# First layer's up and gate products of the feed-forward as block products, seven for eight

## The chip, the cores and the metric

One Trainium2 chip, one core. The metric is the device time of one launch in microseconds; the median of the runs counts.

## The reference, cut to what matters

Two layers over 256 context tokens and 512 latent tokens of width 1024, all in float32. In each layer a mixing sub-layer is followed by a feed-forward sub-layer:

```python
def swiglu(h, w_up, w_down):
    g, u = jnp.split(h @ w_up, 2, axis=-1)
    return (jax.nn.silu(g) * u) @ w_down
...
        x = post_norm(x, gate2 * swiglu(modulate(x, shift2, scale2), ffn_w_up[l], ffn_w_down[l]), ln2_g[l], ln2_b[l])
        if not last:
            xc = post_norm(xc, gate2c * swiglu(modulate(xc, shift2c, scale2c), ffn_w_up[l], ffn_w_down[l]), ln2_g[l], ln2_b[l])
```

`w_up` is 1024 x 5632 (gate columns, then up columns), `w_down` 2816 x 1024. In the first layer both token sets go through (768 tokens), in the last one only the latent tokens (512).

## The kernel before, in words

**Three matmuls for a product.** Every large operand is kept as two float32r tiles, hi (a rounded copy, made by ScalarE) and lo (the rest, made by VectorE). `mm3` (line 240) adds hi x hi, hi x lo and lo x hi in PSUM for each block of 128 along K. `wload` (208) brings weights into `wf` on the sync queue (SP), casts them into `wh` (219) and subtracts into `wl` (220); `wf` has two buffers, `wh` and `wl` four each, of up to 1056 columns. `wchunk` (224) loads 4 K blocks at a time.

**Feed-forward of layer 0** (lines 1486 to 1541). The input `h2` lies channel-major: 8 K blocks x 768 tokens, hi and lo. The hidden width is 22 tiles of 128, in three parts of 8, 7 and 7. For each tile `up` (1498) loads 128 gate and 128 up columns, and `cm` (265) makes, for the latent tokens (512 columns, `LG`) and the context tokens (256, `CG`), the gate product, then Silu on ScalarE (1505), the up product, the multiplication on VectorE (1507) and the hi/lo split into `a` (1509, 1510). After each part `to_tokens` (1254) makes its down products: four column quarters of `w_down`, six token tiles each, `a` as the stationary operand; VectorE multiplies by the gate row (1263) and adds to `X` (1265, 1267). In the last part the normalisation (`fin2`, `post`, `norm_mod`, `modulate`) of a token tile follows its last quarter, and the next layer's first weights are loaded.

**The first two tiles.** Their weights are loaded within the output product of the mixing sub-layer; they are done by column groups (latent first), as the normalised tokens arrive in the order 2, 3, 4, 5, 0, 1 (0 and 1 are context).

**Buffers.** PSUM banks of products alternate between two (`pl`) and three (`pq`) through `pw` (123). `u` (two buffers) holds the normalised tokens and then the gate activations; `lng`, `lnb`, `grow0`, `grow1` hold rows that are broadcast; `hf` (two) the modulated blocks.

**Order.** The code gives an order; the framework that builds the program orders each engine's and queue's instructions by a plan made ahead, taking an instruction when its inputs and buffers are free in that plan, so the order within an engine may differ from the code's. On the chip each engine goes through its own list in order. Modulation vectors of later stages (`ada`, 298, four matmuls and a 512 KB load of `wa` a piece) are slipped in by `pieces`, three per weight chunk in this stage (`NP[2]`).

Of the kernel before, what the change touches and what calls it, by code (L numbers as in the profile page):

```python
# [89 lines left out]
def block_kernel(ctx, tc, t, out, dbg=None):  # L90
# [17 lines left out]
    def nm(s):  # L108
        uid[0] += 1
        return f"{s}_{uid[0]}"  # L110
# [128 lines left out]

    def mm3(po, lhs, rhs):  # L240
        n = len(lhs)
        for k in range(n):
            (ah, al), (bh, bl) = lhs[k], rhs[k]
            mm(po, ah, bh, start=(k == 0), stop=False)  # L244
            mm(po, ah, bl, start=False, stop=False)  # L245
            mm(po, al, bh, start=False, stop=(k == n - 1))  # L246

# [113 lines left out]

    def gate_row(pool, l, which, s):

        g = pool.tile([P, D], F32, tag=f"grow{s}", name=nm("grow"), bufs=1)
# [45 lines left out]

    def modulate(tp, h, i, xhs, fs, nd=0):

        s = 1 if i < 2 else 0
        for k2 in range(0, KT, 2):
            hf = tp.tile([P, 2, 2 * P], F32, tag="hf", name=nm("hf"), bufs=2)
            po = pm().rearrange("p (k s) -> p k s", k=2)
# [836 lines left out]

    def to_tokens(pool, l, which, X, W_of, lhs_of, nk, tiles_, first, final, grows, fin, following):

        def part(t_, W, q):
            mark('w_out' if which == 1 else 'down')
            po = pw()[:, :256]
            mm3(po, lhs_of(t_), W)
            g = grows[1 if t_ < 2 else 0]  # L1260
# [11 lines left out]
        for q in range(2 if final else 4):  # L1272
            W = W_of(q)
            for t_ in tiles_:
# [141 lines left out]
    for l in range(DEPTH):  # L1416
# [7 lines left out]
        with tc.tile_pool(name=f"ff{l}", bufs=1, reuse_waits="tile") as fp:  # L1424
# [8 lines left out]
            for i in tiles_:  # L1433
# [5 lines left out]
                nc.sync.dma_start(X[i], src)  # L1439

            def rows_of(w):
                gr = fp.tile([P, D], F32, tag="lng", name=nm("lng"), bufs=1)
                br = fp.tile([P, D], F32, tag="lnb", name=nm("lnb"), bufs=1)
# [11 lines left out]
            def norm_mod(t_, hdst, f, z):  # L1455

                V = nc.vector
                xh = fp.tile([P, D], F32, tag="u", name=nm("xh"), bufs=2)
                V.tensor_scalar(z[:, 1:2], z[:, 0:1], -1.0 / D, None, op0=ALU.mult)
# [6 lines left out]
                if len(xhs) == 2:  # L1466
                    modulate(fp, hdst, t_ - 1, xhs, f, 4 if t_ in tiles_[-2:] else 0)
# [4 lines left out]
            grows = [gate_row(fp, l, 1, s) if not (last and s == 1) else None for s in range(2)]  # L1472

# [13 lines left out]
            ahead.update(n=NP[2], lim=(l + 1, 2))  # L1487
            gr, br = rows_of(2)
            grows = [gate_row(fp, l, 2, s) if not (last and s == 1) else None for s in range(2)]
            groups = [LG] if last else [LG, CG]  # L1490
            parts = [(0, 8), (8, 7), (15, 7)]
            hn = None
            for pi_, (k0, nk) in enumerate(parts):
                a = new_h(hpool)
                mark('up')
                Wu, ut = {}, {}

                def up(kk, gs_):
                    if kk not in Wu:
                        Wu[kk] = w_up(k0 + kk) if pi_ or kk > 1 else Wn[kk]  # L1500
                        ut[kk] = fp.tile([P, D], F32, tag="u", name=nm("sg"), bufs=2)
                    sg = {}
                    for po, g in cm(Wu[kk], 0, h2, gs_, pw):
                        sg[g] = ut[kk][:, g[0]:g[1]]
                        nc.scalar.activation(sg[g], po, AF.Silu)
                    for po, g in cm(Wu[kk], P, h2, gs_, pw):
                        nc.vector.tensor_tensor(sg[g], po, sg[g], op=ALU.mult)
                        hi = a.t[:, 0, kk, g[0]:g[1]]
                        nc.scalar.copy(hi, sg[g])
                        nc.vector.tensor_tensor(a.t[:, 1, kk, g[0]:g[1]], sg[g], hi.bitcast(F32), op=ALU.subtract)  # L1510
                if pi_ == 0:

                    for g in ((NC_, 512), (512, NT)) + (() if last else (CG,)):
                        up(0, [g])
                        up(1, [g])
                for kk in range(0 if pi_ else 2, nk):
                    up(kk, groups)
                if not last and pi_ == 1:
                    ada_to(l + 1, 2)
                    fsn = shift_scale(l + 1, 1)  # L1520
                if pi_ == 1:
                    ahead["n"] = 0
                final = pi_ == 2
                if final and not last:
                    hn_box = []

                def fin2(t_, st):
                    mark('fin2')
                    z = None if last else sm.tile([P, 5], F32, tag="z", name=nm("z"))
                    post(t_, gr, br, st, None if last else z[:, 0:1])  # L1530
                    if last:
                        nc.sync.dma_start(out[0, (t_ - 2) * P:(t_ - 1) * P, :], X[t_])
                    else:
                        if t_ >= 2:
                            nc.sync.dma_start(xdram[(t_ - 2) * P:(t_ - 1) * P, :], X[t_])
                        if not hn_box:
                            hn_box.append(new_h(hpool2))
                        norm_mod(t_, hn_box[0], fsn, z)
                Wn = to_tokens(fp, l, 2, X, lambda q: wchunk(t["ffn_w_down"][l], [(q * 256, 256)], r0=k0 * P, nk=nk),
                               lambda t_: a.sl(t_ * P, (t_ + 1) * P, 0, nk), nk, tiles_, pi_ == 0, final, grows, fin2,  # L1540
                               lambda n: None if last else wchunk(t["w_in"][l + 1], [((O_AQ, O_AFF)[n], 256)]))
        hg.__exit__(None, None, None)
        if not last:
            h, hg, hpool = hn_box[0], hg2, hpool2

# [31 lines left out]
```

## Time and profile before

| what | us |
|---|---|
| median of 3 runs | 2526.88 (2523.86 to 2527.05) |
| the profiled execution, its own time | 2528.81 |
| its span, first to last instruction | 2526.9 |
| PE busy in the span | 2463.4 (97%) |
| VectorE busy | 1348.1 (53%) |
| ScalarE busy | 875.3 (35%) |
| GpSimd busy | 140.6 (6%) |

PE is the tensor engine, DVE VectorE, ACT ScalarE, POOL GpSimd, SP the sync engine. The profile's page gives busy shares, the chain of work that ended last, and groups of instructions by line. The mean granted clock of PE is 0.992 of full speed. Matmuls overlap, so the spacing of their starts, not the printed length, is what each takes from PE.

### The profile page before, as it was taken

To read this page: it belongs to the slowest core of one execution; us is meant where nothing else is said; L and a number is where in the kernel's file an instruction comes from. 1 tells how busy PE (TensorE), PEld (TensorE's weight loads), DVE (VectorE), ACT (ScalarE), POOL (GpSimd) and SP (SyncE) were. 2 spreads that over 40 slices of the span, in tenths; PEclk is the share of its full clock that TensorE was granted. 3 is DMA by queue.
4 is the path that set the end of the run, shared out by engine and by line. 5 is a ranking of instruction groups with operands and counts; after the bars stand their busy time and mean duration, and the time that the engine had idled before them with its cause. 6 is when DMAs were issued, how large, how long until landed. Compare 5 with 4: busy or idle time off the path is not lost.

```text
span 2526.9 us, 41389 instructions
## 1 busy us (share of the span) xinstructions
PE 2463.4 (97%) x17088; PEld 2108.2 (83%) x17088; DVE 1348.1 (53%) x2896; ACT 875.3 (35%) x1549; POOL 140.6 (6%) x214
## 2 busy tenths in 40 slices
PE   7999999999999999999999999999999999999998
PEld 5878889788678988998998988778887688898987
DVE  4477575445449652232332474768566577443436
ACT  3435553333332242212212144456343423322221
POOL 2000000100100120000000040000010102000000
PEclk9999999999999999999999999999999999999999
DMA  7453122112236444122122164421313265423332
GB/s 247 137 171 118 55 69 80 61 61 97 72 103 202 167 138 145 58 68 67 56 71 59 56 195 142 128 80 59 105 51 112 76 204 184 120 84 101 92 98 78
DMA packets 251936, 269.54 MB, mean 107 GB/s; under 512 B 14972, under 2 KB 219876, under 8 KB 251748
## 3 DMA queue, kind: packets, MB, share of 16 engines
q1 hardware_dynamic: 236867, 238.69, 30.8%
q10 hardware_dynamic: 14880, 28.21, 3.0%
q8 instruction: 134, 2.20, 0.4%
q14 instruction: 55, 0.44, 0.0%
HBM read 238.28 MB, written 26.48 MB: 105 GB/s over the span
## 4 chain that ended last, share of the span: by engine, by line
PE 89%; DVE 4%; DMA 2%; ACT 2%; issue 1%; POOL 1%; SPq 1%; POOLq 0%; ACTq 0%; DVEq 0%
PE pl L244 18%; PE pl L246 17%; PE pl L245 17%; PE pq L245 8%; PE pq L244 8%; PE pq L246 8%; PE po L311 2%; PE po L954 1%; PE pm L942 1%; DMA wa<-in_ada_w_dram 1%; PE pq L1168 1%; PE po L1001 1%; PE pq L1072 1%; DMA wf<-in_w_in_dram 1%; PE pm L989 1%
## 5 line engine op out<-in xcount | busy, mean ns | idle before, releaser
L244 PE MATMUL pl<-h,wh 128*128 128x512 f32 (+1 forms) x1720 | 623.7, 363 | 7.9 <-ACT s L925 2.5
L245 PE MATMUL pl<-h,wh 128*128 128x512 f32 (+1 forms) x1720 | 618.2, 360 | 0.0
L246 PE MATMUL pl<-h,wl 128*128 128x512 f32 (+1 forms) x1720 | 618.1, 359 | 0.0
L220 DVE TENSOR_TENSOR wl<-wf,wh 128x1024 fp32r<-128x1024 f32 (+2 forms) x288 | 348.1, 1209 | 354.0 <-ACT wh L219 339.0
L219 ACT CAST wh<-wf 128x1024 fp32r<-128x1024 f32 (+2 forms) x288 | 298.5, 1037 | 529.2 <-PE pq L246 232.3
L244 PEld LDWEIGHTS pl<-h,wh 128*128 128x128 f32 x1720 | 326.6, 190 | 73.3 <-issue 12.6
L246 PEld LDWEIGHTS pl<-h,wl 128*128 128x128 f32 x1720 | 326.4, 190 | 57.8 <-issue 10.1
L245 PEld LDWEIGHTS pl<-h,wh 128*128 128x128 f32 x1720 | 327.0, 190 | 50.8 <-issue 6.9
L244 PE MATMUL pl<-wh,h 128*128 128x256 f32 (+1 forms) x1048 | 296.2, 283 | 0.6 <-ACT dtr L521 0.4
L245 PE MATMUL pl<-wl,h 128*128 128x256 f32 (+1 forms) x1048 | 296.1, 283 | 0.0
L246 PE MATMUL pl<-wh,h 128*128 128x256 f32 (+1 forms) x1048 | 296.0, 283 | 0.0
L246 PE MATMUL pq<-h,wl 128*128 128x256 f32 (+1 forms) x680 | 219.5, 323 | 0.0
L244 PE MATMUL pq<-h,wh 128*128 128x256 f32 (+1 forms) x680 | 219.3, 323 | 0.0
L245 PE MATMUL pq<-h,wh 128*128 128x256 f32 (+1 forms) x680 | 218.6, 322 | 0.0
L244 PEld LDWEIGHTS pl<-wh,h 128*128 128x128 f32 x1048 | 198.0, 189 | 4.6 <-issue 2.3
L245 PEld LDWEIGHTS pl<-wl,h 128*128 128x128 f32 x1048 | 198.0, 189 | 3.8 <-issue 3.2
L246 PEld LDWEIGHTS pl<-wh,h 128*128 128x128 f32 x1048 | 198.1, 189 | 3.5 <-issue 3.3
L245 PE MATMUL pq<-wl,h 128*128 128x256 f32 x600 | 168.9, 282 | 0.0
L246 PE MATMUL pq<-wh,h 128*128 128x256 f32 x600 | 168.6, 281 | 0.0
L244 PE MATMUL pq<-wh,h 128*128 128x256 f32 x600 | 168.6, 281 | 0.0
L244 PEld LDWEIGHTS pq<-h,wh 128*128 128x128 f32 x680 | 128.0, 188 | 14.1 <-issue 2.6
L245 PEld LDWEIGHTS pq<-h,wh 128*128 128x128 f32 x680 | 128.3, 189 | 13.6 <-issue 1.8
(419 smaller groups left out, 3483.2 us busy)
## 6 DMA issues: line engine op xcount, KB each, us to landing
wf<-in_w_in_dram SPq DMA_DIRECT2D x120, 512.0 KB, 3.5
wa<-in_ada_w_dram SPq DMA_DIRECT2D x96, 512.0 KB, 3.9
wf<-in_ffn_w_up_dram SPq DMA_DIRECT2D x176, 256.0 KB, 3.1
wf<-in_ffn_w_down_dram SPq DMA_DIRECT2D x32, 512.0 KB, 3.3
gsp<-gs ACTq DMA_DIRECT2D x32, 384.0 KB, 2.5
gld<-gsp SPq DMA_DIRECT2D x16, 768.0 KB, 4.8
wf<-in_w_branch_dram SPq DMA_DIRECT2D x16, 512.0 KB, 3.4
wf<-in_w_out_dram SPq DMA_DIRECT2D x16, 512.0 KB, 3.9
```

Of the source, the lines that this page charges most:

```text
L219: nc.scalar.copy(wh[:, :a * b], wf[:, :a * b])
L220: nc.vector.tensor_tensor(wl[:, :a * b], wf[:, :a * b], wh[:, :a * b].bitcast(F32), op=ALU.subtract)
L244: mm(po, ah, bh, start=(k == 0), stop=False)
L245: mm(po, ah, bl, start=False, stop=False)
L246: mm(po, al, bh, start=False, stop=(k == n - 1))
L311: mm(po[32 * j:32 * j + 32, :], cT[:, k].rearrange("p r s -> p (r s)"), wf[:, j * 256:(j + 1) * 256], start=(k == 0), stop=(k == KT - 1))
L942: nc.tensor.transpose(pt[:, (2 * k + j) * P:(2 * k + j + 1) * P], x, ident)
L954: mm(po[hh * 64:hh * 64 + 64, :], va(hh, k), PT[hh][k], start=(k == 0), stop=(k == nk - 1))
L989: nc.tensor.transpose(pt[:, (2 * k + j) * P:(2 * k + j + 1) * P], Pj[j][:, (2 * b + k) * P:(2 * b + k + 1) * P], ident)
L1001: mm(po[hh * 64:hh * 64 + 64, cs], va(hh, k) if k < 2 else va(hh, k - 2, i2 + j), PT[hh][k][:, cs], start=(k == 0), stop=(k == 3))
L1072: mm(out_, q3[rows, u, i * P:(i + 1) * P], k3[rows, u, c0:c1], start=True, stop=True)
L1168: mm(out_, qS[rows, u, i * P:(i + 1) * P], kS[rows, u, c0:c1], start=True, stop=True)
```

## The change

Only layer 0's feed-forward changes in what it computes with; layer 1 keeps its code. Hidden tiles 0 and 1 are made as before. For tiles 2 to 21, two at a time (`k`, `k + 1`), the gate product and then the up product of 256 columns x 1024 x 768 tokens are split into 2 x 2 blocks (128 columns, 512 of K, 384 tokens) and made by `seven`: seven block products instead of eight, with sums of weight blocks before (in place in a raw float32 tile, `w8`), and sums of products after. `split` makes hi and lo of one 512-element block; two of them share a `wh`/`wl` buffer. The four sums of input blocks, `T`, are made once by `t_sums`; one of them replaces the block of `h2` that is not used by itself. The result of each pair (after Silu and multiplication) is stored to a DRAM tile `ad` from the GpSimd queue and read back by `bring` on the SP queue, which makes hi and lo, before and during the down products. The down parts are 8, 8 and 6 tiles long; the first begins with the first four K blocks of four token tiles (`begun`). Gate rows and normalisation rows share the `w8` buffers; the gate rows of the second sub-layer are made at the start of the down products instead of ahead of the up products. One piece of a modulation vector follows each group of seven. `modulate` takes halves of one `hf` tile.

The core of the diff:

```diff
+    def split(x):
+        if pair["n"] % 2 == 0:
+            pair["h"] = wt.tile([P, WN], F32R, tag="wh", name=nm("wh"), bufs=4)
+            pair["l"] = wt.tile([P, WN], F32R, tag="wl", name=nm("wl"), bufs=4)
+        c = 512 * (pair["n"] % 2)
+        pair["n"] += 1
+        hi, lo = (pair[q][:, c:c + 512].rearrange("p (k c) -> p k c", k=4) for q in "hl")
+        nc.scalar.copy(hi, x)
+        nc.vector.tensor_tensor(lo, x, hi.bitcast(F32), op=ALU.subtract)
+        return [(hi[:, k], lo[:, k]) for k in range(4)]
+
+    def t_sums(x, B, T):
...
+        whole(x1, 12)
+        whole(x2, 22)
+        V.tensor_tensor(x3, x2, x1, op=ALU.subtract)
+        put(3, x3)
+        whole(x3, 11)
+        V.tensor_tensor(x1, x1, x3, op=ALU.subtract)
+        put(1, x1)
+        V.tensor_tensor(x2, x2, x1, op=ALU.subtract)
+        put(2, x2)
+        whole(x3, 21)
+        V.tensor_tensor(x3, x2, x3, op=ALU.subtract)
+        put(4, x3)
+
+    def seven(raw, F, cp, out_):
+        V, A = nc.vector, nc.scalar
+        n = cp[0].shape[-1]
+        a11, a12, a21, a22 = (raw[:, 4 * k:4 * k + 4, m * P:(m + 1) * P] for m in range(2) for k in range(2))
+        p1, u2, u3, p5 = cp
+
+        def product(L, name):
+            po = pw()[:, :n]
+            mm3(po, L, F[name])
+            return po
+        L1 = split(a11)
+        A.copy(p1, product(L1, "11"))
+        L22 = split(a22)
+        V.tensor_tensor(a22, a21, a22, op=ALU.add)
+        A.copy(p5, product(split(a22), "t1"))
+        V.tensor_tensor(a21, a11, a21, op=ALU.subtract)
+        V.tensor_tensor(a11, a22, a11, op=ALU.subtract)
+        V.tensor_tensor(u2, p1, product(split(a11), "t2"), op=ALU.add)
+        L3 = split(a21)
+        z = product(L22, "t4")
+        V.tensor_tensor(u3, u2, product(L3, "t3"), op=ALU.add)
+        V.tensor_tensor(u2, u2, p5, op=ALU.add)
+        V.tensor_tensor(out_[3], u3, p5, op=ALU.add)
+        V.tensor_tensor(out_[2], u3, z, op=ALU.subtract)
+        L4 = split(a12)
+        V.tensor_tensor(out_[0], p1, product(L4, "21"), op=ALU.add)
+        V.tensor_tensor(a12, a12, a11, op=ALU.subtract)
+        V.tensor_tensor(out_[1], u2, product(split(a12), "22"), op=ALU.add)
...
+            def w8():
+                return fp.tile([P, 2 * D], F32, tag="w8", name=nm("w8"), bufs=2)
...
+                def store(k, sg):
+                    nc.gpsimd.dma_start(ad[k:k + 2].rearrange("k p s -> p k s"), sg)
...
+                for k in range(2, HID // P, 2):
+                    mark('up')
+                    sg = hidden()
+                    s4 = sg.rearrange("p k (n s) -> p (k n) s", n=2)
+                    for gu in range(2):
+                        raw = raw_of(k, gu) if gu or k > 2 else raw0
+                        cp = fp.tile([P, 2 * NT], F32, tag="hf", name=nm("cp"), bufs=1)
...
+                        seven(raw, F, c4, c4 if gu else [s4[:, q] for q in range(4)])
+                        for m in range(2):
+                            if not gu:
+                                nc.scalar.activation(sg[:, m], sg[:, m], AF.Silu)
+                            else:
+                                nc.vector.tensor_tensor(sg[:, m], cp[:, m * NT:(m + 1) * NT], sg[:, m], op=ALU.mult)
+                        pieces(ahead["n"], ahead["lim"])
+                    store(k, sg)
...
+                def bring(dst, n, k, tl):
+                    mark('down')
+                    st_ = tl()[:, :2 * NT].rearrange("p (k s) -> p k s", k=2)
+                    nc.sync.dma_start(st_, ad[k:k + 2].rearrange("k p s -> p k s"))
+                    hi = dst.t[:, 0, n:n + 2]
+                    nc.scalar.copy(hi, st_)
+                    nc.vector.tensor_tensor(dst.t[:, 1, n:n + 2], st_, hi.bitcast(F32), op=ALU.subtract)
+                parts = [(h2, 0, 8), (T_, 8, 8), (h2, 16, 6)]
+                for n, tl in zip(range(0, 8, 2), (u_tile, w8, w8, u_tile)):
+                    bring(h2, n, n, tl)
+                grows = gate_rows(2)
```

## Rows read from the trace of the kernel before

**Rows 1.** Part 1 of the page: busy time of each engine

```profile
PE 2463.4 (97%) x17088; PEld 2108.2 (83%) x17088; DVE 1348.1 (53%) x2896; ACT 875.3 (35%) x1549; POOL 140.6 (6%) x214
```

**Rows 2.** Part 4 of the page: the chain that ended last

```profile
PE 89%; DVE 4%; DMA 2%; ACT 2%; issue 1%; POOL 1%; SPq 1%; POOLq 0%; ACTq 0%; DVEq 0%
```

**Rows 3.** Table of stretches: us; PE, PEld, DVE, ACT, POOL busy; clock, DMA share, GB/s

```profile
1125.00:1250.00 125.00, 125.00 (x740) 110.59 (x740) 35.09 (x50) 29.34 (x44) 0.00 (x0) 1.00 0.22 65
...
1427.00:1500.00 73.00, 72.90 (x627) 66.75 (x626) 55.23 (x116) 25.38 (x38) 19.94 (x27) 1.00 0.46 147
```

**Rows 4.** Waits of PE, 905 to 1500 us: total, times, longest

```profile
PE po L311 <- DMA wa<-in_ada_w_dram: 3.2, 1, 3.2
```

**Rows 5.** Timeline of ACT: gate activations of second and third part, first and last

```profile
1131.48 0.60 ACT L1505 ACTIVATE sg<-pl 128x512 f32<-128x512 f32 x1 [4.46 <-PE pl L246]
...
1232.00 0.60 ACT L1505 ACTIVATE sg<-pl 128x512 f32<-128x512 f32 x1 [3.99 <-PE pl L246]
...
1308.80 0.60 ACT L1505 ACTIVATE sg<-pl 128x512 f32<-128x512 f32 x1 [4.54 <-PE pl L246]
...
1408.06 0.60 ACT L1505 ACTIVATE sg<-pl 128x512 f32<-128x512 f32 x1 [3.97 <-PE pl L246]
```

**Rows 6.** Timeline of PE, an up tile: from 512 columns to 256

```profile
1156.20 0.39 PE L246 MATMUL pl<-h,wl 128*128 128x512 f32 x1
...
1156.43 0.28 PE L244 MATMUL pq<-h,wh 128*128 128x256 f32 x1
...
1156.55 0.28 PE L245 MATMUL pq<-h,wh 128*128 128x256 f32 x1
```

**Rows 7.** Timeline of DVE, an up tile

```profile
1142.22 1.23 DVE L220 TENSOR_TENSOR wl<-wf,wh 128x1024 fp32r<-128x1024 f32 x1 [0.28 <-ACT wh L219]
1143.36 0.42 DVE L1507 TENSOR_TENSOR sg<-pq,sg 128x256 f32<-128x256 f32 x1
1143.70 1.22 DVE L220 TENSOR_TENSOR wl<-wf,wh 128x1024 fp32r<-128x1024 f32 x1
...
1156.70 0.69 DVE L1507 TENSOR_TENSOR sg<-pl,sg 128x512 f32<-128x512 f32 x1 [11.45 <-PE pl L246]
```

**Rows 8.** Timeline of ACT, the same up tile

```profile
1140.60 0.62 ACT L1509 CAST h<-sg 128x512 fp32r<-128x512 f32 x1 [5.91 <-DVE sg L1507]
...
1142.55 1.06 ACT L219 CAST wh<-wf 128x1024 fp32r<-128x1024 f32 x1 [0.36 <-PE pq L245]
1143.81 0.41 ACT L1509 CAST h<-sg 128x256 fp32r<-128x256 f32 x1 [0.21 <-DVE sg L1507]
1148.21 0.60 ACT L1505 ACTIVATE sg<-pl 128x512 f32<-128x512 f32 x1 [3.99 <-PE pl L246]
```

**Rows 9.** Table of stretches before and behind PE's wait (columns as in rows 3)

```profile
916.40:919.60 3.20, 0.06 (x4) 0.07 (x8) 0.00 (x0) 0.72 (x1) 0.00 (x0) 0.83 0.45 172
919.60:923.00 3.40, 3.40 (x21) 2.26 (x21) 0.55 (x1) 0.00 (x0) 0.00 (x0) 0.50 0.37 101
923.00:926.50 3.50, 3.50 (x28) 2.21 (x27) 2.33 (x4) 2.88 (x5) 1.24 (x2) 0.67 0.52 173
```

**Rows 10.** Timeline of DVE, end of the first sub-layer

```profile
922.45 1.18 DVE L424 TENSOR_SCALAR hf<-pm,modc,modc 128x256 f32<-128x256 f32 x2 [9.06 <-PE pm L420]
...
930.46 0.67 DVE L429 TENSOR_TENSOR h<-hf,h 128x512 fp32r<-128x512 f32 x1
...
951.28 0.42 DVE L1507 TENSOR_TENSOR sg<-pq,sg 128x256 f32<-128x256 f32 x1 [2.87 <-PE pq L246]
```

**Rows 11.** Timelines of SP and ACT queues: a gate load, the last gate store

```profile
715.45 0.89 SPq L1236 DMA_DIRECT2D gld<-gsp  x2
...
754.02 0.33 ACTq L1191 DMA_DIRECT2D gsp<-gs  x1
```

**Rows 12.** Tiles gsp (stored from ACT) and gld (loaded by SP): issue to landing, all

```profile
DMA to landing us min/median/max: 2.0/3.1/6.2
...
DMA to landing us min/median/max: 3.4/4.7/6.2
```

More of the change, by code (lines that the diff above doesn't have):

```diff
@@ L237, in wchunk, with mm3 @@
         return res
-    def mm3(po, lhs, rhs):
+    def mm3(po, lhs, rhs, first=True, final=True):
         n = len(lhs)
@@ L243, in mm3 @@
             (ah, al), (bh, bl) = lhs[k], rhs[k]
-            mm(po, ah, bh, start=(k == 0), stop=False)
+            mm(po, ah, bh, start=(first and k == 0), stop=False)
             mm(po, ah, bl, start=False, stop=False)
-            mm(po, al, bh, start=False, stop=(k == n - 1))
+            mm(po, al, bh, start=False, stop=(final and k == n - 1))
+    pair = {"n": 0}
+    def split(x):
[8 more added lines that the diff above has]
+        return [(hi[:, k], lo[:, k]) for k in range(4)]
@@ new lines, in t_sums, with whole, put @@
+    def t_sums(x, B, T):
+        V = nc.vector
+        x1, x2, x3 = x
+        def whole(x, q):
+            V.tensor_tensor(x, B[q][0].bitcast(F32), B[q][1].bitcast(F32), op=ALU.add)
+        def put(n, x):
+            nc.scalar.copy(T[n][0], x)
+            V.tensor_tensor(T[n][1], x, T[n][0].bitcast(F32), op=ALU.subtract)
+        whole(x1, 12)
[10 more added lines that the diff above has]
+        put(4, x3)
@@ L360, in shift_scale, with gate_row @@
         return (lambda k, s: a[:, l, k, s:s + 1], lambda k, s: b[:, l, k, s:s + 1])
-    def gate_row(pool, l, which, s):
-        g = pool.tile([P, D], F32, tag=f"grow{s}", name=nm("grow"), bufs=1)
+    def gate_row(pool, l, which, s, g=None):
+        if g is None:
+            g = pool.tile([P, D], F32, tag=f"grow{s}", name=nm("grow"), bufs=1)
         row = garow
@@ L1251, in mixing, with to_tokens @@
         return y
-    def to_tokens(pool, l, which, X, W_of, lhs_of, nk, tiles_, first, final, grows, fin, following):
+    def to_tokens(pool, l, which, X, W_of, lhs_of, nk, tiles_, first, final, grows, fin, following, begun=0):
+        pos = {}
         def part(t_, W, q):
             mark('w_out' if which == 1 else 'down')
-            po = pw()[:, :256]
-            mm3(po, lhs_of(t_), W)
+            if t_ in pos:
+                po = pos.pop(t_)
+                mm3(po, lhs_of(t_)[4:], W[4:], first=False)
+            else:
+                po = pw()[:, :256]
+                mm3(po, lhs_of(t_), W)
             g = grows[1 if t_ < 2 else 0]
@@ L1273, in to_tokens @@
             W = W_of(q)
+            if q == 0:
+                for t_ in tiles_[:begun]:
+                    mark('down')
+                    pos[t_] = pw()[:, :256]
+                    mm3(pos[t_], lhs_of(t_)[:4], W[:4], final=False)
             for t_ in tiles_:
@@ L1471, in block_kernel, with gate_rows @@
             gr, br = rows_of(1)
-            grows = [gate_row(fp, l, 1, s) if not (last and s == 1) else None for s in range(2)]
+            def gate_rows(which):
+                if last:
+                    return [gate_row(fp, l, which, 0), None]
+                g = w8()
+                return [gate_row(fp, l, which, s, g[:, s * D:(s + 1) * D]) for s in range(2)]
+            grows = gate_rows(1)
             def fin1(t_, st):
@@ L1486, in block_kernel @@
             ada_to(l + 1, 0)
[L1487 to L1494, printed above, removed]
-                mark('up')
[L1496 to L1541, printed above, removed]
@@ L1542, in block_kernel, with fin2 @@
-        hg.__exit__(None, None, None)
+            ahead.update(n=1, lim=(l + 1, 2))
+            hn_box = []
+            def fin2(t_, st):
+                mark('fin2')
+                z = None if last else sm.tile([P, 5], F32, tag="z", name=nm("z"))
+                post(t_, gr, br, st, None if last else z[:, 0:1])
+                if last:
+                    nc.sync.dma_start(out[0, (t_ - 2) * P:(t_ - 1) * P, :], X[t_])
+                else:
+                    if t_ >= 2:
+                        nc.sync.dma_start(xdram[(t_ - 2) * P:(t_ - 1) * P, :], X[t_])
+                    if not hn_box:
+                        hn_box.append(new_h(hpool))
+                    norm_mod(t_, hn_box[0], fsn, z)
@@ L1543, in block_kernel @@
+        (hg if last else hg2).__exit__(None, None, None)
         if not last:
-            h, hg, hpool = hn_box[0], hg2, hpool2
+            h = hn_box[0]
 _INS = ['x', 'c', 'ctx', 'c_ctx', 'ada_w', 'ada_b', 'w_in', 'hgrn_lb', 'hgrn_norm', 'ssd_conv_w', 'ssd_conv_b',
```

104 lines of the change are left out of this document (98 added, 6 removed).

## The prediction

> **What bounds the kernel now.** First the page: TensorE (PE) is busy for 2463.4 of 2526.9 us [rows 1] and is 89% of the chain that ended last [rows 2]. Then the table of stages, for this change lives in one of them: in the second up stretch of layer 0's feed-forward PE is busy in every microsecond, and VectorE (DVE) in 28% of them [rows 3]. Then PE's waits: from 905 to 1500 us there is one, of 3.2 us, for a load of modulation weights [rows 4]. So a matmul less there is time less, and a new wait there is time lost; nothing hides either. To see what the matmuls cost I read spacings of starts, since matmuls overlap and their "busy" is longer than their share.
>
> **The saving.** Before, a hidden tile of 128 columns needs 8 blocks of K x 3 matmuls x 2 (gate, up) = 48 matmuls over 512 columns and 48 over 256. Twenty such tiles (2 to 21) are 960 + 960, that is 1920 times 384 columns. After, ten pairs of tiles take two groups (gate, up) of seven products of 4 x 3 = 12 matmuls over 384 columns: 1680. Tiles 0 and 1 and all down products keep their matmuls. A hidden tile takes (1232.00 - 1131.48)/6 = 16.75 us in the second part and (1408.06 - 1308.80)/6 = 16.54 in the third [rows 5]; at 16.75 for the first thirteen tiles (those of the first part stand further apart, with other matmuls between them that stay) and 16.54 for seven it is 333.5 us, 0.1737 us per 384 columns. The 240 that go are worth 41.7 us. That rests on a price for a width that the trace lacks. Its bounds are the neighbours: 0.12 us from a matmul of 256 columns to the next start, 0.23 from one of 512 [rows 6]. At these ends the 1680 matmuls would take 202 or 386 us, 132 less or 53 more than now. Both neighbours pay the same per column (0.45 to 0.47 ns), so there is no fixed part to speak of and I take the line between them; an error of 0.002 us each would be 3 us.
>
> **What the other engines take on, in the steady part.** Per pair of groups PE now has 168 x 0.1737 = 29.2 us. DVE gets 14 lo parts and 8 sums of weights at 512 elements, 14 sums of products at 384 and 2 multiplications at 768. Starts of DVE instructions stand 1.14 us apart for 1024 elements and 0.34 for 256 [rows 7], so 0.61, 0.47 and 0.87 on the line: 13.4 + 6.6 + 1.7 = 21.7 us, 74% of PE's time. By the printed durations (0.69 at 512, 0.42 at 256 [rows 7]; 0.56 and 0.96 between and beyond) it is 15.2 + 7.8 + 1.9 = 24.9 us, 85%. Before it was 28%. ScalarE (ACT) gets 14 casts of 0.62, 4 copies of 0.5 (0.41 at 256, 0.62 at 512) and 2 Silu of 0.81 over 768 (0.60 at 512) [rows 8]: 8.7 + 2.0 + 1.6 = 12.3 us, 42%. So PE stays the longest, if the two keep ahead of it.
>
> Here the row and a rule differ. Of two DVE instructions in a row the second starts before the first's printed end: 1143.36 against 1142.22 + 1.23 [rows 7]. The Trainium skill, "VectorE: DVE Perf Modes", section "The DRAIN you can't avoid", says that the next one does not start until the pipe is empty. By the rule the load would be the 85%, by the row 74%; both are below PE, so the sum stays and only the slack differs.
>
> Do they keep ahead? Eight halves of hi/lo buffers serve seven factors: the first two pairs of buffers are free after the third and fourth products, four to five products (8 to 10 us) before the next group's second product, whose chain (cast, lo, sum, cast, lo) is about 3.1 us. PSUM gives five banks to products of 2.1 us that are read at once. The one tile for partial results delays the first copy of a group by at most 0.5 + 1.7 us after the last product, while PE is in the next product. And the order on the queues is not that of the program: the second cast for the next tile's weights ran at 1142.55, ahead of the cast of the running tile's second half at 1143.81 that stands before them in the code [rows 8]. I take 0.15 us of loss per group, 3 us; ends 0 and 16 (0.8 per group, which is a DVE instruction in the way each time). Weights are loaded raw, 1 MB per group in two issues where there were four per tile; with a store and a vector's weights it is some 130 GB/s, against 147 in the last down part [rows 3]. Costed at nothing: the double buffer hides 4 to 5 us of load behind 14.6 us of products. The modulation pieces (one per group) keep their matmuls.
>
> **The start.** Four sums T are new: twelve DVE instructions over 1536 elements at 1.67 (the line again) and four casts of some 1.5. The context half of the input is ready at 931.1 [rows 10]; one of the two plain sums fits into DVE's idle 9 us before 922.45 [rows 10], the rest wait for buffers that the context tiles' modulation holds until 931. From there the chain to T4 is nine DVE steps and about three uncovered casts, 20 us, and 2 to 6 us of other DVE work between: 953 to 957. PE has products of tiles 0 and 1 until 951.2, less 2 us (16 matmuls of 256 columns for gate rows, now later), then three products (6.3 us) before it needs T4: 955.5. I take 2 us of wait; ends -6 (the wait at 916 and the half clock behind it go) and +6.
>
> **The end.** Results now go to DRAM on POOL's queue, 11 stores of 786 KB, and come back on SP's, 11 loads; the hi/lo split moves from the up part to the down part at the same number of elements. A store waits for the second multiplication of its pair; POOL has nothing queued behind it there. Eight tiles come back before the first down product. The first four overwrite a block that is free after the fourth product of the last group, 6.3 us ahead. The other four wait for the last product: two casts (3.0 us) beside out1, two multiplications and two lo parts on DVE (0.5 + 1.7 + 3.4), 5.6 us, covered by 48 matmuls begun on four token tiles (48 x 0.117 = 5.6 us). The last load waits for a buffer and would be late by 1 to 2 us. On SP's queue that load stands in the code ahead of the first down weights; if it is issued so, these come late by about 5 us (load, cast, lo). I take 2 us; ends 0 and 14 (third rival). That loads wait only for their own part of a DRAM tile shows in the merge: loads of the gates were issued at 715.45, stores of other gates until 754.02 [rows 11].
>
> **The tail.** The parts of the down products are 8, 8, 6 tiles for 8, 7, 7, so 24 x 3 matmuls (8.3 us) leave the last part, where the normalisation runs: PE 72.9 of 73.0 us, DVE 55.2 [rows 3]. DVE's spare 18 us take most of it. I take 1.5 us; ends 0 and 4.
>
> **Sum.** -41.7 + 3 + 2 + 2 + 1.5 = -33.2 us against the profiled execution's 2528.81 (span 2526.9 and 1.9 around it): 2495.6. The median of the runs is 1.9 lower, 2526.88: **2493.7, say 2494 us.** The forecast's own range is 2485 (nothing lost) to 2504.
>
> **Rivals.**
> 1. *DVE is in the way.* Casts and lo parts pass between ACT and DVE fourteen times per pair, and DVE waits in order: in the profile its longest waits are for PE (11.45 us before a sum [rows 7]). If a product's sum stands before a needed lo part each time, 0.8 us per group go: 2494 + 13 = 2507. For it: 74 to 85% load. Against: deadlines of four products. 0.13.
> 2. *Slower: the border of the groups.* If the queues keep the order of the code, the next group's factors come only after the last sum: 0.5 + 0.9 (half of the two multiplications) + cast 0.6 + lo 0.7 = 2.7 us without PE, then 0.9 and 0.3 before the second and third product, 3.9 us for each of 20 groups, 78 us; with the other terms 2527 - 41.7 + 5.5 + 78 = 2569. It decides from (41.7 - 5.5)/20 = 1.8 us per group. Against it stands the early cast [rows 8]. 0.06.
> 3. *The hand-over.* If the first down part waits for the last store's round trip: 0.5 + 1.7 of sums, a store of 3.1 to 6.2, a load of 4.7 [rows 12], cast and lo 3.2, so 13 to 16 us less 2 to 3 of other work. A wait of that length costs clock as well: behind the 3.2 us in which PE stood, it was granted 0.50 (1.2 of 2.4 GHz) for 3.4 us and 0.67 in the next 3.5 [rows 9], 1.7 + 1.2 = 2.9 us lost. 2494 - 2 + 12 + 3 = 2507. No row has a store from POOL's queue, which speaks for it; the merge's rows against. 0.08.
> 4. *It does not do what it says:* a 384-column matmul costs the next size up, 0.23 us: 1680 of them take 386 us, 53 more: 2526.9 + 53 + 8 = 2588. The equal price per column speaks against it. 0.02.
>
> **Chances.** The forecast has 0.71. A measurement of this kernel can tell about 0.2%, 5 us, from no change. Faster by more: forecast, 1 and 3 but for their worst ends, 0.90; within it 0.03; slower 0.07 (2 and 4 nearly alone). The range takes the forecast's own, 1 us of the start's possible gain, and rivals 1 and 3 with some of their spread: 2484 to 2511.
>
> **What would show it.** Right: 1680 matmuls of 384 columns at starts 0.174 us apart, the two groups of a pair 29 us apart, PE's waits in the up part below 10 us, DVE at 75 to 85% there, a wait of a few us at the first group and at the first down part. Wrong: starts of 384-column matmuls off the line; a wait of the same size at each border, with DVE or ACT as its releaser (1, 2); a long wait for a load of the hidden tiles (3); granted clock below 1 in the up part.

## The result, and the profile after

The changed kernel takes **2492.78 us** (median of 4 runs, 2488.32 to 2493.98), the kernel before beside it 2525.37 (4 runs, 2522.59 to 2527.05): ratio 0.9861, 95% interval 0.9847 to 0.9876. A second measurement, beside the later runs, gave 2493.76 and 0.987 (0.9852 to 0.9888). The forecast was 2494 in 2484 to 2511. The profiled execution took 2492.36, with a span of 2490.4.

Page, parts 1 and 4 (before: [rows 1, 2]): busy time of each engine, and the chain that ended last.

```profile
PE 2427.9 (97%) x16848; PEld 2113.8 (85%) x16848; DVE 1516.3 (61%) x3173; ACT 928.7 (37%) x1638; POOL 149.7 (6%) x225
...
PE 89%; DVE 3%; ACT 2%; DMA 2%; issue 1%; POOL 1%; SPq 1%; POOLq 0%; ACTq 0%; DVEq 0%
```

240 matmuls fewer, 277 VectorE instructions more, the same chain. What it cost or gave is read from the stage. This table of stretches of the changed kernel (columns as in [rows 3]) shows the up part and the last down part:

```profile
1000.00:1200.00 200.00, 200.00 (x1158) 198.65 (x1157) 151.04 (x257) 79.37 (x136) 5.08 (x7) 1.00 0.31 103
...
1390.00:1460.00 70.00, 69.34 (x605) 63.51 (x603) 57.05 (x124) 21.70 (x33) 18.64 (x24) 1.00 0.51 158
```

PE is busy in all of the 200 us, as before, and DVE in 76% instead of 28% [rows 3]. All waits of PE from 905 to 1480 us (the stretch of [rows 4]):

```profile
PE po L386 <- DMA wa<-in_ada_w_dram: 2.1, 3, 1.2
PE pm L496 <- ACT u L1563: 1.1, 2, 0.9
PE pl L245 <- ACT u L1664: 0.4, 1, 0.4
```

None of the three lines belongs to the block products: loads of modulation weights, two waits for normalised tokens (L1563), and one for a Silu of the first two tiles (L1664). The price of the new width, in PE's timeline (before: [rows 6]), and the copy of the first product of every second group, in ACT's:

```profile
1130.01 0.34 PE L247 MATMUL pl<-h,wl 128*128 128x384 f32 x1
1130.18 0.34 PE L245 MATMUL pl<-h,wh 128*128 128x384 f32 x1
```

```profile
1109.63 0.48 ACT L305 COPY cp<-pl 128x384 f32<-128x384 f32 x1 [1.37 <-PE pl L247]
...
1226.72 0.48 ACT L305 COPY cp<-pl 128x384 f32<-128x384 f32 x1 [1.39 <-PE pl L247]
```

Starts are 0.174 us apart. A pair of groups takes (1226.72 - 1109.63)/4 = 29.27 us, which is 168 x 0.1742: the printed length of 0.34 is twice what a matmul takes from PE.

Now the span in three: up to DVE's first read of the mixing sub-layer's output product, the feed-forward of layer 0, and layer 1 from its first activation. One table for each execution (columns as in [rows 3]). Before, the execution of the rows ahead of the prediction, then a second one (of that, from 837.87 on):

```profile
0.00:833.24 833.24, 801.76 (x5907) 664.04 (x5908) 483.03 (x1175) 330.77 (x662) 40.33 (x77) 1.00 0.36 115
833.24:1521.43 688.19, 683.59 (x4900) 617.92 (x4898) 287.97 (x519) 176.71 (x257) 53.14 (x75) 1.00 0.31 96
1521.43:2526.90 1005.47, 978.10 (x6284) 826.21 (x6284) 577.11 (x1202) 367.80 (x631) 47.11 (x62) 0.99 0.34 107
```

```profile
837.87:1525.98 688.11, 682.95 (x4900) 617.45 (x4898) 287.88 (x519) 176.66 (x258) 52.50 (x75) 1.00 0.32 96
1525.98:2526.90 1000.92, 974.42 (x6284) 824.04 (x6284) 576.78 (x1202) 367.48 (x631) 46.98 (x62) 0.99 0.36 107
```

After, the execution of the lines above, then one from the second measurement (from 840.23 on):

```profile
0.00:840.79 840.79, 810.20 (x5907) 670.97 (x5908) 482.84 (x1176) 330.59 (x662) 40.24 (x77) 0.98 0.37 114
840.79:1483.58 642.79, 638.37 (x4660) 614.60 (x4658) 456.06 (x796) 230.89 (x347) 62.64 (x86) 1.00 0.40 129
1483.58:2490.40 1006.82, 979.33 (x6284) 828.25 (x6284) 577.35 (x1202) 367.26 (x631) 46.80 (x62) 0.99 0.35 107
```

```profile
840.23:1486.05 645.82, 639.40 (x4660) 615.91 (x4658) 456.09 (x796) 231.00 (x346) 64.94 (x86) 1.00 0.40 129
1486.05:2492.80 1006.75, 979.57 (x6284) 827.98 (x6284) 577.60 (x1202) 366.92 (x631) 46.79 (x62) 0.99 0.35 107
```

The feed-forward became shorter by 45.4 us (688.2 to 642.8) in the first pair and by 42.3 (688.1 to 645.8) in the second. In the first execution before, 3.4 us of the stretch were lost to half clock behind its wait of 3.2 us [rows 9]; in the second pair 1.7 us were lost on both sides. Without them the two pairs give 42.0 and 42.3. The changed kernel's span is 36.5 and 34.1 us shorter: 8 us of the gain are not there at the end, though the other two stretches hold the same matmuls (5907 and 6284). Where they went is taken up below.

### The profile page after: what moved, and what is told of

Its sections match the earlier page's. It is cut to its first block, busy times and chain, and to the rows that moved or that the text cites. A ratio compares the mean times of both kernels' runs of the same rounds, so it can differ in the third digit from the quotient of the medians.

```text
span 2490.4 us, 41350 instructions
## 1 busy us (share of the span) xinstructions
PE 2427.9 (97%) x16848; PEld 2113.8 (85%) x16848; DVE 1516.3 (61%) x3173; ACT 928.7 (37%) x1638; POOL 149.7 (6%) x225
## 4 chain that ended last, share of the span: by engine, by line
PE 89%; DVE 3%; ACT 2%; DMA 2%; issue 1%; POOL 1%; SPq 1%; POOLq 0%; ACTq 0%; DVEq 0%
PE pl L245 17%; PE pl L247 17%; PE pl L246 17%; PE pq L245 8%; PE pq L247 8%; PE pq L246 8%; PE po L386 1%; DMA wa<-in_ada_w_dram 1%; PE po L1030 1%; PE pm L1018 1%; PE pq L1244 1%; DMA wf<-in_w_in_dram 1%; PE po L1077 1%; PE pq L1148 1%; PE pm L1065 1%
## 5 line engine op out<-in xcount | busy, mean ns | idle before, releaser
L245 PE MATMUL pl<-h,wh 128*128 128x512 f32 (+2 forms) x1680 | 593.2, 353 | 9.9 <-ACT dtr L597 2.6
L247 PE MATMUL pl<-h,wl 128*128 128x512 f32 (+2 forms) x1680 | 587.1, 350 | 0.0
L246 PE MATMUL pl<-h,wh 128*128 128x512 f32 (+2 forms) x1680 | 586.8, 349 | 0.3 <-DVE h L505 0.3
L220 DVE TENSOR_TENSOR wl<-wf,wh 128x1024 fp32r<-128x1024 f32 x248 | 299.1, 1207 | 316.2 <-ACT wh L219 315.3
L219 ACT CAST wh<-wf 128x1024 fp32r<-128x1024 f32 x248 | 256.2, 1035 | 475.0 <-PE pq L247 195.2
L245 PEld LDWEIGHTS pl<-h,wh 128*128 128x128 f32 x1680 | 320.3, 191 | 61.8 <-issue 11.7
L247 PEld LDWEIGHTS pl<-h,wl 128*128 128x128 f32 x1680 | 320.2, 191 | 44.2 <-issue 9.5
L246 PEld LDWEIGHTS pl<-h,wh 128*128 128x128 f32 x1680 | 320.9, 191 | 37.7 <-issue 5.8
L245 PE MATMUL pq<-h,wh 128*128 128x384 f32 (+2 forms) x640 | 224.8, 352 | 0.0
L247 PE MATMUL pq<-h,wl 128*128 128x384 f32 (+2 forms) x640 | 223.9, 351 | 0.0
L246 PE MATMUL pq<-h,wh 128*128 128x384 f32 (+2 forms) x640 | 223.6, 350 | 0.0
L245 PEld LDWEIGHTS pq<-h,wh 128*128 128x128 f32 x640 | 120.3, 188 | 12.9 <-issue 2.9
L247 PEld LDWEIGHTS pq<-h,wl 128*128 128x128 f32 x640 | 120.2, 188 | 12.6 <-issue 2.0
```

What stands on the lines that cost most here:

```text
L219: nc.scalar.copy(wh[:, :a * b], wf[:, :a * b])
L220: nc.vector.tensor_tensor(wl[:, :a * b], wf[:, :a * b], wh[:, :a * b].bitcast(F32), op=ALU.subtract)
L245: mm(po, ah, bh, start=(first and k == 0), stop=False)
L247: mm(po, al, bh, start=False, stop=(final and k == n - 1))
```

## The experiments

All ratios are to the kernel before, run on the same chip. "The changed kernel" is 2493 us.

**Eight products for seven.** All else of the change stays (blocks of 384 tokens, raw weights, the DRAM tile, begun down products), but the four block results are summed in PSUM:

```diff
-        L1 = split(a11)
-        A.copy(p1, product(L1, "11"))
...
+        Ls = [split(x) for x in (a11, a12, a21, a22)]
+        for m in range(2):
+            for q in range(2):
+                po = pw()[:, :n]
+                mm3(po, Ls[2 * m] + Ls[2 * m + 1], F[f"1{q + 1}"] + F[f"2{q + 1}"])
+                (V.tensor_copy if q else A.copy)(out_[2 * m + q], po)
...
-                t_sums(x, B, T)
```

> Eight block products for each group in place of seven, each pair of them summed in PSUM over 24 matmuls; no sums of weights, no T, one copy of each result; store, read-back, buffers and down parts as in the change. PE then has the matmuls of the kernel before, in 384 columns. Theory (the gain is the twelfth of a group's products that is left out, at 0.174 us a matmul): 20 x 12 x 0.174 = 41.8 us above the change, about 2534.6. Rival (the rest of the change costs or gives nothing, and seven's own sums lose the 7 to 9 us between 41.8 and what was measured): equal to the kernel before, 2525, so only 33 above the change.

2530.35 us, ratio 1.0008 (0.9997 to 1.002). By the ratios that is 37 us above the changed kernel, between the theory's 41.8 and the rival's 33, so the median alone does not decide. The stretch does (columns as in [rows 3]):

```profile
833.39:1519.95 686.56, 680.19 (x4900) 655.68 (x4898) 302.04 (x544) 188.35 (x282) 62.76 (x86) 1.00 0.38 121
```

The feed-forward took 686.6 us, against 688.2 before. So in this stretch moving the results through DRAM, the raw loads, the later gate rows and the other split of the down parts together cost nothing that can be measured, and give nothing. The gain is in making seven products for eight: 686.6 - 642.8 = 43.8 us in the stretch, and 685.4 - 645.8 = 39.6 in the second executions of both, against 240 x 0.174 = 41.8.

**VectorE's room: each lo part made twice, then three times.**

```diff
-        nc.vector.tensor_tensor(lo, x, hi.bitcast(F32), op=ALU.subtract)
+        for _ in range(2):
+            nc.vector.tensor_tensor(lo, x, hi.bitcast(F32), op=ALU.subtract)
```

> Each of a group's seven lo parts is computed twice: 7 x 512 elements more for DVE per group, same result. Theory (DVE has the slack that its starts show, 0.605 us each): 10.85 + 4.24 = 15.1 us of DVE for about 15.0 of PE, so 0 to 8 us more: 2493 to 2501. Rival (an instruction takes DVE its whole printed length, 0.69): 12.45 + 4.83 = 17.3 us, 2.3 over PE, 20 groups: 46 us more, about 2539.

> Each lo part three times: 14 x 512 elements more per group. DVE is now the bound under both. Theory (starts, 0.605): 10.85 + 8.47 = 19.3 us for 15.0, 4.3 more per group, 86 us: about 2579. Rival (printed lengths, 0.69): 12.45 + 9.66 = 22.1, 7.1 more, 142 us: about 2635.

Twice: 2516.34 us, 0.9955 (0.9935 to 0.9975), by the ratios 24 us more than the changed kernel. Three times: 2580.61, 1.0196 (1.0178 to 1.0213), 85 more. Table of stretches (columns as in [rows 3]) and the largest sum of waits of PE (930 to 1400 us), lo parts made twice, then three times:

```profile
1000.00:1200.00 200.00, 193.30 (x1092) 189.39 (x1091) 197.31 (x339) 76.79 (x134) 4.35 (x6) 1.00 0.27 90
```

```profile
PE pl L245 <- ACT cp L306: 5.4, 8, 1.1
```

```profile
1000.00:1200.00 200.00, 168.74 (x862) 157.21 (x862) 198.99 (x342) 57.52 (x102) 3.65 (x5) 0.95 0.23 78
```

```profile
PE pq L247 <- DVE wl L266: 24.6, 17, 2.4
```

With three, DVE is busy in 199 of 200 us and sets the pace: 38.69 us a pair (mean of seven pairs, by the copies of the first product). By starts DVE would need 21.7 + 28 x 0.605 = 38.6 us, by printed lengths 24.9 + 28 x 0.69 = 44.2. The measurement is the former. So the 74% of the prediction was DVE's load, and not the 85%. The Trainium skill, "VectorE: DVE Perf Modes", section "The DRAIN you can't avoid", has the next instruction start only when the pipe is empty, but says in the same paragraph that one that is not held starts earlier. The prediction took the first half alone; this trace goes by the second, with 0.605 us between starts of instructions printed as 0.69.

With two, the pair takes 30.65 us (seven pairs), near the 30.2 by starts, but the time is 24 us longer and not 0 to 8. The first two pairs, behind the T sums, took 42.1 and 34.1 us where the changed kernel has 34.7 and 29.2 (12.3 us), and the next seven lose 8.0 in sum: DVE has no room left to catch up with them. In the profile the feed-forward stretch took 661.1 us, 18 more than the changed kernel's 642.8; the rest of the 24 lies outside it and goes with the granted clock (0.988 in the mean of its five runs, 0.992 in the changed kernel's). What was missing in that expectation is the size of a piece of work that comes at once. Here a full engine that is not PE cost little by its rate and much at a start.

**The border of the groups.** The second rival made real: the next group's weights are made to depend (by a sum of zero in 16 columns) on the last sum of the group before.

```diff
+        if pair["z"] is not None:
+            ends = raw.rearrange("p k (m c) -> p k m c", m=2)[:, :, :, 0:1]
+            V.tensor_tensor(ends, ends, pair["z"].unsqueeze(1).unsqueeze(3).to_broadcast([P, 8, 2, 1]), op=ALU.add)
...
+        V.tensor_scalar(pair["z"], out_[1][:, 0:2], 0.0, None, op0=ALU.mult)
```

> Zero times the last sum of a group is added to one element of each block of the next group's raw weights before they are split (one DVE instruction of 16 elements, one of 2), so that all of a group's factors are made behind the last sum of the group before: the order of the code at the border of the groups, rival 2 of the prediction. If that order were what the change has, nothing changes: 2493. Theory (the plan makes the factors some products ahead, and that is what hides them): 3.9 us of PE's time per group by the working of rival 2, 19 borders: 74 us, about 2567; PE's waits at each border with ACT or DVE as releaser.

2554.15 us, 1.0101 (1.0087 to 1.0116): 61 us more than the changed kernel. PE's waits, 930 to 1400 us, and the stretch:

```profile
PE pl L245 <- ACT wh L264: 22.5, 9, 2.5
PE pq L245 <- ACT wh L264: 20.1, 9, 2.2
```

```profile
1000.00:1200.00 200.00, 172.99 (x903) 164.52 (x902) 130.81 (x229) 63.20 (x111) 3.62 (x5) 0.95 0.22 73
```

2.4 us at each of 18 borders listed (2.7 worked out in the rival), and the granted clock falls to 0.95 on average. So the rival's first price was right and its side too; the further 0.9 and 0.3 us it had for the second and third product are not in the list. In this profile the feed-forward stretch itself took 717.9 us, 75 more than 642.8 (74 were expected): 20 of them were lost to half clock, and the other two stretches were 13 us shorter, 8 of them by the clock. It did not happen in the changed kernel because there the plan takes the next group's factors between the last sums, as this timeline of its DVE at a border shows (L265 is a lo part of the next group, L315 a sum of the old one):

```profile
1130.40 0.69 DVE L265 TENSOR_TENSOR wl<-w,wh 128x512 fp32r<-128x512 f32 x1
1131.01 0.55 DVE L315 TENSOR_TENSOR cp<-cp 128x384 f32<-128x384 f32 x1
1131.48 0.68 DVE L265 TENSOR_TENSOR wl<-w,wh 128x512 fp32r<-128x512 f32 x1
```

**Nothing begun ahead of the down products** (`begun` 4 becomes 0 for the first part).

```diff
-                                   grows, fin2, lambda n: wchunk(...), 0 if pi_ else 4)
+                                   grows, fin2, lambda n: wchunk(...), 0)
```

> The changed kernel with the first down products in the plain order: no products of the first four K blocks are begun ahead. Theory: the last two of eight hidden tiles come back from DRAM 4 to 6 us after the last up product, and only the begun products cover them: a wait of TensorE of 3 to 5 us before the first down products, with up to 3 us of clock behind it, 2496 to 2501. Rival: the other work there (the gate rows' matmuls, the first four K blocks of one token tile) covers it anyway: the time of the changed kernel.

2491.3 us, 0.9864 (0.9846 to 0.9882), beside 0.987 (0.9852 to 0.9888) for the changed kernel on that chip: no cost, the rival was right. PE's waits from 1230 to 1300 us are an empty list. In this kernel's timeline the gate rows and several half-done products fill the place:

```profile
1248.83 1.89 PE L446 MATMUL pm<-garow,ident 128*128 128x256 f32 x8
1250.37 0.47 PE L245 MATMUL pq<-wh,h 128*128 128x256 f32 x1
...
1252.68 0.28 PE L245 MATMUL pl<-wh,h 128*128 128x256 f32 x1
```

A second product starts at 1252.68 while the first (begun at 1250.37) is not done; the plan begins products ahead without being told to, in the five PSUM banks. The written-out order was not what covered the hand-over.

**The same in layer 1**, to see where the idea ends. 512 tokens make products of 256 columns, so PE's time per group falls by a third, and DVE's work on weights stays. First with all sums on DVE, then with the four weight sums of each group on GpSimd. The edit: `if last:` and its up part go, token counts become `NS = NT - T0`, and `seven` gets the engine of the weight sums:

```diff
-    def seven(raw, F, cp, out_):
+    def seven(raw, F, cp, out_, S):
...
-        V.tensor_tensor(a22, a21, a22, op=ALU.add)
+        S.tensor_tensor(a22, a21, a22, op=ALU.add)
```

> Layer 1's up and gate products made the same way (512 tokens, so block products of 256 columns), all sums on VectorE. TensorE saves 240 more matmuls of 256 columns, 240 x 0.1165 = 28.0 us; a group is 84 x 0.1165 = 9.8 us for it. VectorE per group, by starts: 11 operations of 512 elements at 0.605 (7 lo parts, 4 sums of weights), 7 sums at 256 at 0.34 and a multiplication of 512 = 9.6 us, 98% of TensorE's time; the four T sums (12 operations of 1024 at 1.14, 13.6 us) come on top. Theory (what the run with doubled lo parts showed): with no slack the T sums are a backlog that is never made up, so the gain is 28 less 12 to 20: 8 to 16 us under the changed kernel, about 2480. Rival: the orders of the queues cost as soon as VectorE is full, no gain or a loss, 2493 or more.

> As the run before, but the four sums of weight blocks of each of layer 1's groups are made by GpSimd. VectorE has then 7.2 us per group of 9.8 (74%, the load that layer 0 has in the changed kernel). Theory: TensorE is the bound again and most of the 28.0 us is saved, 20 to 26 us under the changed kernel, about 2470. Rival: VectorE's operations become longer while GpSimd works (0.82 instead of 0.42 us beside it in the kernel before) or GpSimd's sums come too late: no better than the run before.

On DVE alone: **2481.43 us**, 0.9826 (0.9811 to 0.9841), 12 under the changed kernel. With GpSimd: 2498.43, 0.9893 (0.9878 to 0.9908), 5 over it: the rival. Stores of finished pairs from GpSimd's queue show the pace. For all sums on DVE: the stores, two stretches (columns as in [rows 3]), and PE's longest wait there:

```profile
2134.54 0.78 POOL L1617 DMA_DIRECT2D ad<-u  x1 [11.71 <-DVE u L1627]
2168.38 0.74 POOL L1617 DMA_DIRECT2D ad<-u  x1 [33.06 <-DVE u L1661]
2188.43 0.73 POOL L1617 DMA_DIRECT2D ad<-u  x1 [19.30 <-DVE u L1661]
```

```profile
2135.00:2145.00 10.00, 5.52 (x22) 4.94 (x23) 9.49 (x10) 4.37 (x5) 0.32 (x1) 0.57 0.77 261
2200.00:2250.00 50.00, 50.00 (x422) 50.00 (x421) 48.16 (x96) 24.81 (x48) 2.18 (x3) 1.00 0.44 146
```

```profile
PE pq L245 <- ACT h L277: 4.1, 1, 4.1
```

The size came as expected, the mechanism did not: from the second pair on, PE goes at its own pace, 20.05 us = 168 x 0.1193, beside a DVE that is busy in 96% of the time. The loss is at the start alone: the first pair took 33.8 us, with a wait of 4.1 us for T (L277 is its cast), around which the granted clock is 0.57 in the mean, most of it the lower of its two levels (1.2 of 2.4 GHz).

With the weight sums on GpSimd a pair took 22.2 us, no less than two plain tiles of the changed kernel's layer 1 (2 x 11.1). The groups of lines there (2000 to 2280 us; all on DVE, then with GpSimd) tell why; the last column but one is the mean in ns:

```profile
L265 DVE TENSOR_TENSOR wl<-w,wh 128x512 fp32r<-128x512 f32 x101 | 67.5, 687 | 0.4 <-ACT wh L264 0.3
L315 DVE TENSOR_TENSOR cp<-cp 128x256 f32<-128x256 f32 x13 | 5.5, 420 | 0.0
```

```profile
L310 POOL TENSOR_TENSOR w<-w 128x512 f32<-128x512 f32 x14 | 23.2, 1659 | 1.1
...
L265 DVE TENSOR_TENSOR wl<-w,wh 128x512 fp32r<-128x512 f32 x94 | 85.1, 925 | 13.8 <-ACT wh L264 13.0
L315 DVE TENSOR_TENSOR cp<-cp 128x256 f32<-128x256 f32 x13 | 15.4, 1187 | 0.2
```

A sum on GpSimd takes 1.66 us instead of 0.69, and DVE's own instructions become longer beside it: 0.42 us to 1.19. Not all do. Two stretches of the timelines, GpSimd above, DVE below:

```profile
2166.14 1.29 POOL L309 TENSOR_TENSOR w<-w 128x512 f32<-128x512 f32 x1
2167.51 1.63 POOL L310 TENSOR_TENSOR w<-w 128x512 f32<-128x512 f32 x1
```

```profile
2166.74 1.23 DVE L265 TENSOR_TENSOR wl<-w,wh 128x512 fp32r<-128x512 f32 x1 [1.80 <-ACT wh L264]
2167.90 0.41 DVE L314 TENSOR_TENSOR cp<-cp,pl 128x256 f32<-128x256 f32 x1
2168.34 1.07 DVE L315 TENSOR_TENSOR cp<-cp 128x256 f32<-128x256 f32 x1
2169.34 0.41 DVE L316 TENSOR_TENSOR u<-cp 128x256 f32<-128x256 f32 x1
```

The sum of an SBUF tile and PSUM (L314) runs beside GpSimd's L310 at its usual 0.41; the two with both inputs in SBUF (L265, L315) end at 2167.97 and 2169.41, 0.3 to 0.5 us behind the ends of L309 (2167.43) and L310 (2169.14), and L316, of the same kind but with GpSimd idle from 2169.14, takes 0.41 again. The Trainium skill, "SBUF — State Buffer", section "Who interferes with whom", says that a DVE instruction with two SBUF inputs contends with a GpSimd instruction that reads SBUF; the trace agrees. Moving the sums cost 2.2 us in a pair of 20. How much of that is DVE's longer instructions and how much the chain of sum, cast and lo part, which waits for the slower sums (the lo parts of L265 waited 13.0 us for their casts instead of 0.3), was not separated.

**Four plain tiles in layer 1.** The version with all sums on DVE, with tiles 2 and 3 of layer 1 made plainly, so that PE has something to do while the T sums are made:

```diff
+                if last:
+                    sg = hidden()
+                    W2 = [w_up(kk) for kk in (2, 3)]
...
+                    store(2, sg)
+                k1 = 4 if last else 2
...
-                for k in range(2, HID // P, 2):
+                for k in range(k1, HID // P, 2):
```

> The version with block products in both layers (all sums on VectorE), but in layer 1 the hidden tiles 2 and 3 are made plainly too, so that TensorE has 22 us more of work that needs no T sums. Theory: what layer 1 lost is at its start alone (the pair of groups there took 33.8 us between stores where the later ones take 20.0; a wait of 4.1 us for T and 10.2 us at half clock behind it); with the chain covered that is saved, less 2.4 us for 24 more products of 256 columns saved before: 6 to 11 us under that version, about 2473. Rival: VectorE at 96% of its time has no room anywhere, the chain is only pushed back and the loss comes later: the same time or 2.4 us more.

**2472.39 us**, 0.979 (0.9776 to 0.9803): 9 under the version above, 20 under the changed kernel. Its stores of the first and second pair:

```profile
2174.85 0.73 POOL L1617 DMA_DIRECT2D ad<-u  x1 [25.32 <-DVE u L1672]
2193.76 0.72 POOL L1617 DMA_DIRECT2D ad<-u  x1 [18.18 <-DVE u L1672]
```

The wait for T is gone (of PE's waits from 2040 to 2340 us one alone is over 1 us, 1.5 for a modulation load), and the later pairs stay at 20.0 us. So the loss was the start's, and the work of one engine that comes at once wants cover by another's. This version beats both kernels.

**The changed kernel once more,** and **before** and **eight products** once more, unchanged, for the 8 us.

> The changed kernel unchanged, timed beside the runs below. Theory: the 240 matmuls and two removed waits are the whole gain (the stretch of layer 0's feed-forward became shorter by 43.8 to 45.4 us in the traces), and what the medians lack of it is the granted clock in code that did not change: a ratio between 0.982 and 0.987. Rival: a loss that is always there in the rest of the program, some 8 us: 0.986 or 0.987 again, with the same stretches at half clock in the same places.

> The kernel before, looked at once more. The changed kernel came into layer 0's feed-forward 7.0 and 7.6 us later than it in two profiles, with half clock at the same five places ahead of it. Theory: the places belong to the program: this profile has again few falls ahead of the feed-forward (two of 3.4 us) and reaches its first down read of the output product at 833 us. Rival: they differ from one execution to the next: other places, 833 to 841 us.

> The version with eight products in a group, looked at once more. Its first profile had no falls of the clock between the first 40 us and 640 us and came to the feed-forward at 833.4 us. Theory: the places belong to the program: the same again, 833 to 834 us. Rival: they differ from one execution to the next: other places, up to 841 us.

The changed kernel: 2493.76, 0.987 (0.9852 to 0.9888), and half clock at the same five places ahead of the feed-forward, which looked like the program's own loss. The other two kernels then showed that, ahead of the feed-forward, it is not. The second execution of before came to the feed-forward at 837.9 instead of 833.2 us, with half clock at four of those places; eight products at 840.4 instead of 833.4, at all five. PE's waits from 20 to 835 us are alike in seven profiles (17.5 to 20.1 us in sum); whether the clock falls behind one differs from execution to execution. Taken without what the clock lost there (3.4, 10.2, 13.7 and 10.2 us), the four tables above have 829.8, 827.7, 827.1 and 830.0 us: no difference that goes with the kernel.

The rest is in layer 1: 1005.5 and 1000.9 us before, 1006.8 twice after. Without what the clock lost there (14.0, 10.4, 11.1 and 11.0 us) it is 991.5, 990.5, 995.6 and 995.8: 4 to 5 us that are there in both executions after. So the rival of the first of these three expectations was right for about half of its 8 us. The version with eight products has them too (995.2 and 995.1), so they come with the program around the block products and not with seven for eight. ACT's timeline shows a part of it. These are activations five tiles apart, in layer 1's up part, before and after:

```profile
2178.24 0.60 ACT L1505 ACTIVATE sg<-pl 128x512 f32<-128x512 f32 x1 [2.29 <-PE pl L246]
...
2233.35 0.60 ACT L1505 ACTIVATE sg<-pl 128x512 f32<-128x512 f32 x1 [4.16 <-PE pl L246]
```

```profile
2137.34 0.60 ACT L1628 ACTIVATE u<-pl 128x512 f32<-128x512 f32 x1 [2.17 <-PE pl L247]
...
2192.88 0.60 ACT L1628 ACTIVATE u<-pl 128x512 f32<-128x512 f32 x1 [4.26 <-PE pl L247]
```

A tile of 48 matmuls takes 11.02 us before and 11.11 after (the second executions: the same), with the same instructions at full clock. Over 20 tiles that is 1.7 us. Layer 1's 2431 matmuls of 256 columns (half clock and pauses left out) start 0.117 us apart in the mean in both executions before, and 0.119 in both after and in both of eight products, which makes some 5 us. It is not the chip: on one chip a tile took 11.02 us with eight products and 11.11 with lo parts made three times. Why the same matmuls start further apart was not tried and stays open.

## Why the prediction was right

**The saving** was its main step, and right: 0.174 us for the 384-column matmul against 0.1737, on the line between its neighbours [rows 6]. With that price, 240 matmuls are 41.8 us; the stretch lost 42.0 and 42.3 with half clock taken out, 45.4 and 42.3 as it stands. The fourth rival (a 384-column matmul at the price of 512) falls with the same rows.

**The losses** were over-estimated, all four: 3 + 2 + 2 + 1.5 = 8.5 us were put down and the stretch shows none. Two signs that the prediction named for being right, a wait of a few us at the first group and one at the first down part, did not appear. *Steady*: no wait at a border, 29.27 us a pair for 29.2 worked out. *Start*: T4 was ready at 956.0, but that it lies in the 953 to 957 worked out is chance, since this execution came into the feed-forward at 840.8 us and not at 833.2. From the context half (ready at 934.1) to T4 it took 21.9 us, the short end of the 22 to 26 worked out. The first block product began at 951.3, so three of them reached to 957.5, and PE had no wait. On top of that 32 matmuls of modulation pieces and their 1.2 us of wait for a load ran between the first products; these were counted as work that stays, and not as cover. *End*: 48 begun matmuls were taken as the cover; the gate rows and products that the plan began by itself cover as much, as the run without them shows, and the four later tiles' lo parts were all done by the time of the last multiplication, as this timeline of DVE shows (L1714 the last lo part, L1700 the multiplications):

```profile
1254.94 1.75 DVE L1714 TENSOR_TENSOR h<-u,h 128x1536 fp32r<-128x1536 f32 x1
...
1258.22 1.81 DVE L1700 TENSOR_TENSOR u<-cp,u 128x768 f32<-128x768 f32 x2
```

The first down part holds tiles 0 to 7, stored long before; only free blocks were waited for. So the store of the last pair, from which the third rival's round trip starts, is not on the path. *Tail*: PE is busy in 69.34 of 70 us with DVE at 57.05; the 1.5 us put down for it are not seen.

**The number** is thus nearer than its steps, and that is luck. 2494 met 2492.8 because some 8 us of loss that did not come stand against some 8 us that the rest of the program ran longer: clock falls that also come without the change, and the 4 to 5 us in layer 1, which no step of the prediction had.

**First rival** (DVE in the way): it did not happen at DVE's 76%, but the runs with more lo parts show where it would: at 99% the rate holds and a start costs over 10 us. **Second**: shown above, the right side and 61 us where 78 were worked out; the plan's order is what keeps it away. Its weight of 0.06 rested on one early cast [rows 8], and that was a fair sign.

## What to carry to other kernels

Where one engine is busy in every microsecond, a matmul less is time less at the spacing of starts, and more work on another engine cost nothing as long as that one kept ahead (VectorE did at 76% and at 96%, not at 99%); but a piece of it that must be done at once, ahead of a first consumer, wants cover (here two more plain tiles, worth 9 us). Sums moved from VectorE to GpSimd were no relief here, where most of VectorE's work has two SBUF inputs. Before a few us are laid to a change, look at the same stretch in two executions of each kernel: here the clock alone moved an unchanged one by 7.

## What was not expected of the hardware

- VectorE instructions beside GpSimd sums: 0.42 us became 1.19 and 0.69 became 0.93 in the mean with two SBUF inputs, while those with one input in PSUM stayed at 0.41.
- The granted clock falls behind waits in some executions and not in others with the same waits: 833.4 and 840.4 us for the same kernel (eight products).
- The same layer 1 tile at full clock takes 11.02 us in one program and 11.11 in the other, twice each, and the cause is open.
